# First unit's norm by sums that leave TensorE on all partitions, and its first loads on two queues

## The chip, the cores and the metric
One core of a Trainium2 chip runs the whole program. The metric is device time in microseconds of one execution; three runs of the kernel before gave 672.42, 673.34 and 673.81 us, median 673.34. Besides these there is one profiled execution, from which every duration below is read. Its engines are TensorE (PE, with weight loads as PEld), VectorE (DVE), ScalarE (ACT), GpSimd (POOL) and SyncE (SP), which issues loads.

## The reference
One layer of a diffusion backbone over 2048 latent positions and 256 context positions of width 1024, all in f32:

```python
mod = silu(c) @ w_ada + b_ada            # shift, scale, gate
h   = rmsnorm(x, gain) * (1 + scale) + shift      # the same for ctx with c_ctx
uf, gf, ul, gl = split(h @ w_in)         # 512 columns each
yf = real(fft2(uf)) @ w_four             # over positions and group channels
yl = bidirectional gated linear recurrence(conv4(ul)), started from the context's final state
x  = x + gate * (concat(yf * silu(gf), yl * silu(gl)) @ w_out)
out = rmsnorm(x, final_gain)
```

The change lies in the first `rmsnorm`: x times the reciprocal root of the mean square of its 1024 features plus 1e-6.

## The kernel before, in words
The latent positions are cut into four units of 512, the context is a fifth. In stage one a unit's x is held transposed: features on the 128 partitions, in four tiles (xt) of two feature blocks each, the 512 positions along the row. For each of the eight feature blocks k a unit goes through: x times the position's reciprocal root (`prep_x`), scale and shift by the modulation gn, sh (`prep_hi`, which gives h and its rounded part hl), the remainder of the split (`prep_lo`), a fold of h for the Fourier group (`fold_x`, eo), a store of h, the products pul with the weights wu (`mms_ul`) and ptt with the Fourier weights wf (`mms_tt`). Products in f32 are made from three rounded partial products (`mm3`).

During the first unit the weights are prepared too. For each k the adaLN block goes through part (`ada_part`), a copy psb, small sums o (`ada_sum`) and the additions that give sh and gn (`ada_fin`); the raw weight wr goes through wu and, by way of the matmuls pw (`four_mm`), through wf.

For units 1 to 3 and the context, the position sums of squares come from a second, untransposed load of x, whose squares ACT sums along the row. The first unit has no such load. Its squares are made from the xt tiles: ACT squares seven of the eight blocks, DVE the eighth; DVE adds blocks 0 to 3 into one tile, 4 and 5 into a second and 6 and 7 into a third (`square0`, `sum0`). TensorE then sums over partitions (`col0`): the tile of squares is the stationary operand, two columns of ones move, and the sums of 128 positions land on 128 partitions, four groups for 512 positions. Root and reciprocal (`stats`) are thus 4 columns wide. `spread` brings them back along the row: matmuls pr against the identity copy each value over all partitions. The first multiply reads pr in PSUM; `spread_copy` puts it into SBUF for the other seven.

The engines' order is written by hand: stage one is the list S1, whose words name operation, unit and block: X load of xt, a load of an adaLN block, w load of a weight, 1 square, + add, 3 column sum, ! warm-up matmul of TensorE with ones, 2 and 4 small ACT operations that also load its tables, A part, b psb, c o, d sh and gn, T root and reciprocal, P spread, x, h, l as above, i pw, m pul. Each engine takes its instructions in that order. SP issues nearly all loads, its queue in order; ACT issues only the load of the small vectors at the start. PSUM holds eight buffers in stage one, which these products take in turn.

Of the kernel before, what the change touches and what calls it, by code (L numbers as in the profile page):

```python
# [52 lines left out]
def tile_layer(ctx, tc, xp, xnat, xt_in, ctxn, ctxt, w_ada, vec, bgate, fgain, w_in, w_g, w_four, w_gate, w_out,  # L53
               dct, d512, rmat, csts, out):
    nc = tc.nc
# [11 lines left out]
    def r(ap):  # L67
        return ap.bitcast(F32)
# [23 lines left out]
    eps_r = const.tile([P, 1], F32, name="eps_r")  # L92
    b1 = const.tile([P, KD], F32, name="b1")
# [9 lines left out]
    p1 = p1stack.enter_context(tc.tile_pool(name="p1", bufs=1, reuse_waits="tile"))  # L103
# [3 lines left out]
    ident = p1.tile([P, P], F32, name="ident", tag="ident")  # L107
    ones_r = p1.tile([P, P], F32R, name="ones_r", tag="onesr")
# [85 lines left out]
    sts = {}  # L194
# [27 lines left out]
    def stats(u):  # L222
        n = 2 if u == "c" else 4
        st = p1.tile([P, 8], F32, name="st0", tag="st", bufs=3) if u == 0 else sts.pop((u, "st"))
        if u == 0:
            nc.scalar.activation(out=st[:, 4:4 + n], in_=sts["ss"][:, 0:2 * n:2], func=AF.Sqrt, scale=1.0 / D, bias=eps_t)
        else:
            nc.scalar.activation(out=st[:, 4:4 + n], in_=st[:, 0:n], func=AF.Sqrt, scale=1.0 / D, bias=eps_t)
        nc.vector.reciprocal(out=st[:, 0:n], in_=st[:, 4:4 + n])
        if u == 0:  # L230
            sts[u] = st
            return
        dgs = []
        if u:
            sr = p1.tile([P, 2, 4], F32R, name=f"sr{u}", tag="sr", bufs=2)
            nc.vector.tensor_copy(sr[:, 0, 0:n], st[:, 0:n])
            nc.vector.tensor_tensor(out=sr[:, 1, 0:n], in0=st[:, 0:n], in1=r(sr[:, 0, 0:n]), op=ALU.subtract)
            for s in range(2):
                dg = p1.tile([P, 4, P], F32R, name=f"dg{u}_{s}", tag="dg", bufs=2)
                nc.vector.tensor_tensor(out=dg[:, 0:n], in0=ident.unsqueeze(1).to_broadcast([P, n, P]),  # L240
                                        in1=r(sr[:, s, 0:n]).unsqueeze(2).to_broadcast([P, n, P]), op=ALU.mult)
                dgs.append(dg)
# [196 lines left out]
    nc.scalar.activation(out=eps_r, in_=eps_t, func=AF.Silu)  # L439
# [28 lines left out]
    def soft_abs():  # L468
# [6 lines left out]
        "!": warm_up, "0": const_loads, "9": small_loads, "1": square0, "+": sum0, "3": col0, "r": lambda: spread_copy(0),  # L475
# [17 lines left out]
    p2 = p2s.enter_context(tc.tile_pool(name="p2", bufs=1, side="right", reuse_waits="tile"))  # L493
# [4 lines left out]
    w4 = [fp.tile([P, 2, 512], F32R, name=f"w4_{j}", tag="w4", bufs=4) if j != 2 else  # L498
          fp.tile([P, 512], F32R, name="w4_2", tag="w42", bufs=1) for j in range(5)]
# [149 lines left out]
    X0 = CTX + GAP  # L649
# [371 lines left out]
    xs, pos, s3 = {}, {}, {}  # L1021
# [7 lines left out]
    p3 = tail.enter_context(tc.tile_pool(name="p3", bufs=1, reuse_waits="tile"))  # L1029
# [195 lines left out]
```

## Time and profile before

| | |
|---|---|
| median of three runs | 673.34 us |
| profiled execution | 675.62 us, span 673.5 us |
| TensorE busy | 659.3 us, 98% |
| VectorE busy | 477.2 us, 71% |
| ScalarE busy | 402.9 us, 60% |
| mean granted TensorE clock | 0.982 |
| HBM read, written | 91.24 MB, 38.27 MB |

Busy time of TensorE counts records whose ends are modelled, so 98% does not say that it runs at its peak; the granted clock beside it says whether it ran at 2.4 GHz (1.00) or 1.2 GHz (0.50). "Idle before" is the time for which an engine did nothing ahead of an instruction, with what released it. The chain follows the program back from its last instruction to what each step waited for.

### The profile page before, as it was taken

To read this page: it belongs to the slowest core of one execution; us is meant where nothing else is said; L and a number is where in the kernel's file an instruction comes from. 1 tells how busy PE (TensorE), PEld (TensorE's weight loads), DVE (VectorE), ACT (ScalarE), POOL (GpSimd) and SP (SyncE) were. 2 spreads that over 40 slices of the span, in tenths; PEclk is the share of its full clock that TensorE was granted. 3 is DMA by queue.
4 is the path that set the end of the run, shared out by engine and by line. 5 is a ranking of instruction groups with operands and counts; after the bars stand their busy time and mean duration, and the time that the engine had idled before them with its cause. 6 is when DMAs were issued, how large, how long until landed. Compare 5 with 4: busy or idle time off the path is not lost.

```text
span 673.5 us, 10726 instructions
## 1 busy us (share of the span) xinstructions
PE 659.3 (98%) x4124; PEld 578.8 (86%) x4124; DVE 477.2 (71%) x771; ACT 402.9 (60%) x578; POOL 105.4 (16%) x170
## 2 busy tenths in 40 slices
PE   8999999999989999999999999999999999999996
PEld 7888888888978889997998989989988888888885
DVE  3768999877646676487879899888989455544513
ACT  4475787556634455668587876887753455543502
POOL 0000201022130113333212222031210000000000
PEclk8899999999997999999999999999999999999998
DMA  9987785639695895344444353342479567774211
GB/s 339 396 315 260 222 293 170 238 94 283 133 328 174 246 315 149 127 126 115 151 116 145 106 184 110 111 141 73 139 254 338 199 219 234 239 255 177 93 63 62
DMA packets 69898, 130.21 MB, mean 193 GB/s; under 512 B 7090, under 2 KB 39986, under 8 KB 69848
## 3 DMA queue, kind: packets, MB, share of 16 engines
q1 hardware_dynamic: 51080, 82.36, 37.7%
q0 software_dynamic: 12384, 39.00, 17.7%
q10 hardware_dynamic: 6384, 8.18, 3.7%
q8 instruction: 32, 0.52, 0.3%
q14 instruction: 18, 0.15, 0.1%
HBM read 91.24 MB, written 38.27 MB: 192 GB/s over the span
## 4 chain that ended last, share of the span: by engine, by line
PE 92%; DMA 3%; ACT 2%; DVE 1%; issue 1%; SPq 0%; DVEq 0%; ACTq 0%
PE po L71 9%; PE pg L71 9%; PE po L72 9%; PE po L73 9%; PE pg L73 9%; PE pg L72 9%; PE pul L71 5%; PE pul L73 4%; PE pul L72 4%; PE ptt L71 2%; PE ptt L73 2%; PE ptt L72 2%; PE pl L72 2%; PE pl L73 2%; PE pl L71 2%; DMA w4a<-in_w_four_dram 1%
## 5 line engine op out<-in xcount | busy, mean ns | idle before, releaser
L71 PE MATMUL pg<-hg,wg 128*128 128x256 f32 x512 | 144.2, 282 | 0.7 <-ACT bs L636 0.7
L73 PE MATMUL pg<-hg,wg 128*128 128x256 f32 x512 | 143.8, 281 | 0.0
L72 PE MATMUL pg<-hg,wg 128*128 128x256 f32 x512 | 143.5, 280 | 0.0
L71 PE MATMUL po<-wo,y 128*128 128x512 f32 (+1 forms) x264 | 102.4, 388 | 0.0
L72 PE MATMUL po<-wo,y 128*128 128x512 f32 (+1 forms) x264 | 102.3, 387 | 0.0
L73 PE MATMUL po<-wo,y 128*128 128x512 f32 (+1 forms) x264 | 102.3, 387 | 0.0
L71 PEld LDWEIGHTS pg<-hg,wg 128*128 128x128 f32 x512 | 96.3, 188 | 4.0 <-ACT wg L544 1.1
L72 PEld LDWEIGHTS pg<-hg,wg 128*128 128x128 f32 x512 | 96.3, 188 | 0.7
L73 PEld LDWEIGHTS pg<-hg,wg 128*128 128x128 f32 x512 | 96.4, 188 | 0.0
L424 POOL DMA_DIRECT2D g_d<-gs x80 | 57.7, 723 | 138.4 <-ACT gs L744 63.3
L71 PEld LDWEIGHTS po<-wo,y 128*128 128x128 f32 x264 | 49.9, 189 | 11.0
L73 PEld LDWEIGHTS po<-wo,y 128*128 128x128 f32 x264 | 49.6, 188 | 11.2
L72 PEld LDWEIGHTS po<-wo,y 128*128 128x128 f32 x264 | 49.6, 188 | 10.7
L71 PE MATMUL pul<-hl,wu 128*128 128x512 f32 x124 | 49.9, 402 | 0.0
L1068 ACT ACTIVATE j<-xr 128x1024 bf16<-128x1024 f32 x15 | 15.9, 1057 | 55.6 <-DVE xr L1063 55.6
L73 PE MATMUL pul<-hl,wu 128*128 128x512 f32 x124 | 49.0, 395 | 0.0
L72 PE MATMUL pul<-hl,wu 128*128 128x512 f32 x124 | 48.8, 394 | 0.0
L838 ACT ACTIVATE g<-pl,vecs 128x1024 f32<-128x1024 f32 x32 | 35.5, 1116 | 14.3 <-PE pl L73 14.2
L287 ACT ACTIVATE h<-xt,sh,gn 128x512 f32<-128x512 f32 x31 | 25.2, 813 | 19.8 <-DVE gn L149 10.4
L71 PE MATMUL ptt<-wf,eo 128*128 128x260 f32 (+1 forms) x128 | 36.5, 286 | 0.0
L73 PE MATMUL ptt<-wf,eo 128*128 128x260 f32 (+1 forms) x128 | 36.3, 283 | 0.0
L72 PE MATMUL ptt<-wf,eo 128*128 128x260 f32 (+1 forms) x128 | 36.2, 283 | 0.0
(297 smaller groups left out, 1475.6 us busy)
## 6 DMA issues: line engine op xcount, KB each, us to landing
xt<-in_xt_dram SPq DMA_DIRECT2D x16, 512.0 KB, 5.4
blk<-in_w_ada_dram SPq DMA_DIRECT2D x16, 512.0 KB, 6.9
hr<-h_d SPq DMA_DIRECT2D x32, 256.0 KB, 4.2
xr<-in_xnat_dram SPq DMA_DIRECT2D x16, 512.0 KB, 3.8
g<-g_d SPq DMA_DIRECT2D x15, 512.0 KB, 5.4
out_dram<-xr POOLq DMA_DIRECT2D x15, 512.0 KB, 2.9
dm<-in_dct_dram POOLq DMA_DIRECT2D x12, 514.0 KB, 6.8
x<-in_xp_dram SPq DMA_DIRECT2D x12, 512.0 KB, 5.1
```

Of the source, the lines that this page charges most:

```text
L71: nc.tensor.matmul(out_, lh, rh, start=first, stop=False, skip_group_check=skip)
L72: nc.tensor.matmul(out_, lh, rl, start=False, stop=False, skip_group_check=skip)
L73: nc.tensor.matmul(out_, ll, rh, start=False, stop=last, skip_group_check=skip)
L287: nc.scalar.activation(out=h[:, 0:n], in_=x, func=AF.Identity, scale=g, bias=b)
L424: queue.dma_start(dst[:, :, row:row + s1 - s0], s[:, :, P * i - off + s0:P * i - off + s1])
L838: nc.scalar.activation(out=t[:, c0:c0 + cn], in_=pg[:, 0:cn], func=AF.Sigmoid, bias=vecs[:, q:q + 1])
L1068: nc.scalar.activation(out=junk, in_=xs[b][t], func=AF.Square, accum_out=s3[b, t][:, 0:1])
```

## The change
Four things are edited, all for the first unit. The column sums take the ones as the stationary operand and move the 512 columns of squares, so each of 128 partitions holds all 512 sums. Root and reciprocal are 512 wide, on that tile, and give rb itself. The spread's matmuls and rb's copy go. The second and fourth xt tile are loaded from ACT's queue; the small Silu that loads ACT's first table is put behind these issues (the word 8). In S1 the words P0 and r go and T0 comes behind b0.

```diff
-S1 = "X0.0 X0.1 X0.2 X0.3 9 a0.0 ... 32 A0 T0 P0 b0 x0.0 c0 d0 u0 h0.0 U0 a2.1 l0.0 f0.0 i0 e0.0 s0.0 r o0.0 ...
+S1 = "X0.0 X0.1 X0.2 X0.3 8 9 a0.0 ... 32 A0 b0 T0 c0 x0.0 d0 u0 h0.0 U0 a2.1 l0.0 f0.0 i0 e0.0 s0.0 o0.0 ...
...
     def load_xt(u, q):
-        nc.sync.dma_start(t[:, :, 0:n], ...)
+        queue = nc.scalar if u == 0 and q % 2 else nc.sync
+        queue.dma_start(t[:, :, 0:n], ...)
...
     def col0(j):
         if j == 0:
             sts["ss"] = ps1.tile([P, 512], F32, name="ss", tag="tr")
-        acc = sts["sq", (0, 4, 6)[j]]
-        for i in range(4):
-            nc.tensor.matmul(sts["ss"][:, 2 * i:2 * i + 2], acc[:, P * i:P * i + P], ones[:, 0:2],
-                             start=j + i == 0, stop=j == 2, skip_group_check=True)
+        nc.tensor.matmul(sts["ss"], ones, sts["sq", (0, 4, 6)[j]], start=j == 0, stop=j == 2)
...
     def stats(u):
         n = 2 if u == "c" else 4
-        st = p1.tile([P, 8], F32, name="st0", tag="st", bufs=3) if u == 0 else sts.pop((u, "st"))
         if u == 0:
-            nc.scalar.activation(out=st[:, 4:4 + n], in_=sts["ss"][:, 0:2 * n:2], func=AF.Sqrt, scale=1.0 / D, bias=eps_t)
...
+            t = rb[0] = p1.tile([P, 512], F32, name="rb0", tag="rb", bufs=2)
+            nc.scalar.activation(out=t, in_=sts["ss"], func=AF.Sqrt, scale=1.0 / D, bias=eps_t)
+            nc.vector.reciprocal(out=t, in_=t)
+            return
...
     def spread(u):
-        if u == 0:
-            for i in range(4):
-                nc.tensor.matmul(pr[:, P * i:P * i + P], sts[0][:, i:i + 1].to_broadcast([P, P]), ident, start=True, stop=True)
...
-        if u:
-            spread_copy(u)
+        spread_copy(u)
...
-    nc.scalar.activation(out=eps_r, in_=eps_t, func=AF.Silu)
...
+        "8": lambda: nc.scalar.activation(out=eps_r, in_=eps_t, func=AF.Silu),
```

The order of instructions shows it at three places. On ACT, at the program's start, before (vecs is the load of the small vectors, eps_r the table-loading operation, sq the squares):

```order
L76 DMA vecs<-in_vec_dram 128x92
L439 ACT_TABLE_LOAD
L439 ACTIVATE eps_r<-eps_t 128x1
L202 ACTIVATE sq_168<-xt_0_129 128x512
L202 ACTIVATE sq_170<-xt_0_129 128x512
```

and after:

```order
L76 DMA vecs<-in_vec_dram 128x92
L185 DMA xt_1_130<-in_xt_dram 128x1024
L185 DMA xt_3_134<-in_xt_dram 128x1024
L466 ACT_TABLE_LOAD
L466 ACTIVATE eps_r<-eps_t 128x1
L203 ACTIVATE sq_168<-xt_0_128 128x512
```

Two tile loads now stand between the vector load and the table load. On TensorE, from the last column sum (ss) to the first products of the unit (pul), before:

```order
L213 MATMUL ss<-ones,sq_185 128x2 x4
L131 MATMUL part_214<-blk_0_139,sc_pad 32x256 x4
L131 MATMUL part_214<-blk_1_141,sc_pad 32x256 x4
L250 MATMUL pr_226<-ident,st_223 128x128 x4
L143 MATMUL o_0_234<-cst,psb_231 128x2
L144 MATMUL o_0_234<-cst,psb_231 128x2
L169 MATMUL pw_251<-rmi,wr_143 128x128 x3
```

and after:

```order
L212 MATMUL ss<-sq_185,ones 128x512
L131 MATMUL part_205<-blk_0_139,sc_pad 32x256 x4
L131 MATMUL part_205<-blk_1_141,sc_pad 32x256 x4
L143 MATMUL o_0_219<-cst,psb_214 128x2
L144 MATMUL o_0_219<-cst,psb_214 128x2
L169 MATMUL pw_237<-rmi,wr_143 128x128 x3
```

The spread pr is gone, and one wide matmul stands for four narrow ones. On DVE, from the last add of squares to the operand of the first pul, before:

```order
L206 TENSOR_TENSOR sq_185<-sq_185,sq_187 128x512
L229 RECIPROCAL st_223<-st_223 128x4
L137 COPY psb_231<-part_214 128x256
L272 TENSOR_TENSOR xt_0_129<-xt_0_129,pr_226 128x512
L148 TENSOR_SCALAR sh<-o_0_234,vecs 128x2
L149 TENSOR_SCALAR gn<-o_0_234,b_82,vecs 128x2
```

and after:

```order
L207 TENSOR_TENSOR sq_185<-sq_185,sq_187 128x512
L137 COPY psb_214<-part_205 128x256
L225 RECIPROCAL rb_216<-rb_216 128x512
L263 TENSOR_TENSOR xt_0_128<-xt_0_128,rb_216 128x512
L148 TENSOR_SCALAR sh<-o_0_219,vecs 128x2
L149 TENSOR_SCALAR gn<-o_0_219,b_82,vecs 128x2
```

The reciprocal has moved behind psb, and 512 columns stand where 4 stood.

## Rows read from the trace of the kernel before
**Rows 1.** The page, chain that ended last: shares of the span by engine

```profile
PE 92%; DMA 3%; ACT 2%; DVE 1%; issue 1%; SPq 0%; DVEq 0%; ACTq 0%
```

**Rows 2.** Windows: stretch, its length, busy by engine, granted clock, DMA share, GB/s

```profile
1.00:4.00 3.00, 2.94 (x14) 2.95 (x15) 0.36 (x4) 1.49 (x2) 0.65 (x1) 1.00 0.65 144
5.00:7.50 2.50, 2.50 (x23) 2.34 (x21) 1.10 (x3) 2.07 (x4) 0.00 (x0) 1.00 1.04 413
...
11.00:12.00 1.00, 1.00 (x6) 0.92 (x6) 0.14 (x1) 0.36 (x2) 0.00 (x0) 0.55 1.01 414
12.00:21.00 9.00, 9.00 (x47) 7.42 (x48) 4.08 (x10) 2.08 (x4) 0.60 (x1) 0.50 1.03 418
21.00:22.00 1.00, 1.00 (x6) 0.85 (x5) 0.69 (x1) 1.00 (x3) 0.00 (x0) 0.83 1.01 414
...
199.00:209.00 10.00, 9.18 (x31) 7.34 (x31) 6.40 (x15) 4.04 (x11) 1.08 (x2) 0.50 0.78 257
```

**Rows 3.** Timeline, loads and squares: start, length, instruction, idle before and releaser

```profile
0.74 1.80 SPq L184 DMA_DIRECT2D xt<-in_xt_dram  x4
...
6.58 1.23 ACT L202 ACTIVATE sq<-xt 128x512 f32<-128x512 f32 x2 [0.16 <-DMA xt<-in_xt_dram]
...
7.86 1.15 ACT L202 ACTIVATE sq<-xt 128x512 f32<-128x512 f32 x2
...
8.80 1.05 PE L213 MATMUL ss<-ones,sq 128*128 128x2 f32 x8 [1.27 <-DVE sq L206]
9.04 0.69 DVE L206 TENSOR_TENSOR sq<-sq,sq 128x512 f32<-128x512 f32 x1 [0.30 <-ACT sq L202]
9.22 0.63 ACT L202 ACTIVATE sq<-xt 128x512 f32<-128x512 f32 x1 [0.21 <-DMA xt<-in_xt_dram]
...
10.44 0.69 DVE L206 TENSOR_TENSOR sq<-sq,sq 128x512 f32<-128x512 f32 x1
...
11.19 1.87 PE L213 MATMUL ss<-ones,sq 128*128 128x2 f32 x8
```

**Rows 4.** Timeline, from the root to the first pul, as rows 3

```profile
12.99 1.93 PE L131 MATMUL part<-blk,sc_pad 128*32 128x256 f32 x16
13.10 0.26 ACT L226 ACTIVATE st<-ss,eps_t 128x4 f32<-128x4 f32 x1 [1.73 <-PE ss L213]
...
14.85 2.08 PE L250 MATMUL pr<-ident,st 128*128 128x128 f32 x8
14.99 0.42 DVE L137 COPY psb<-part 128x256 f32<-128x256 f32 x1 [1.42 <-PE part L131]
...
16.96 0.69 DVE L272 TENSOR_TENSOR xt<-xt,pr 128x512 f32<-128x512 f32 x1 [1.55 <-PE pr L250]
...
17.43 2.38 PE L169 MATMUL pw<-rmi,wr 128*128 128x128 f32 x10
...
18.05 0.81 ACT L284 ACTIVATE hl<-xt,sh,gn 128x512 fp32r<-128x512 f32 x1 [4.18 <-DVE gn L149]
...
19.56 2.45 PE L334 MATMUL pul<-hl,wu 128*128 128x512 f32 x6
```

**Rows 5.** Groups of DVE by shape, reciprocals: count, busy us, mean ns, idle before

```profile
L1076 DVE RECIPROCAL s<-s 128x1 f32<-128x1 f32 x15 | 2.5, 165 | 32.1 <-ACT s L1072 32.1
L229 DVE RECIPROCAL st<-st 128x4 f32<-128x4 f32 x4 | 0.7, 177 | 2.3 <-ACT st L226 2.3
L443 DVE RECIPROCAL sp<-sp 128x8 f32<-128x8 f32 x1 | 0.2, 191 | 0.0
```

**Rows 6.** DMA queues in 2 to 5 us: packets, MB, share (q1 SP, q10 ACT)

```profile
q1 hardware_dynamic: 200, 0.75, 83.6%
q10 hardware_dynamic: 144, 0.05, 7.6%
```

**Rows 7.** Groups of ACT by shape, as rows 5: 512 columns with a scale operand

```profile
L535 ACT ACTIVATE w<-w4a,cst 128x512 fp32r<-128x512 f32 x2 | 1.4, 722 | 7.0 <-DVE w4a L532 7.0
```

**Rows 8.** Timeline of TensorE at the second low stretch, as rows 3

```profile
199.82 0.58 PE L71 MATMUL pz<-dm,S 128*126 128x256 f32 x1 [2.91 <-DVE z L617]
```

More of the change, by code (lines that the diff above doesn't have):

```diff
@@ new lines @@
+S1 = "X0.0 X0.1 X0.2 X0.3 8 9 a0.0 a0.1 w0 0 70 !21 10 11 +1 12 13 +2 +3 2 14 15 +5 16 17 4 +7 w1 30 a1.0 a1.1 a2.0 !1 31 !1 32 A0 b0 T0 c0 x0.0 d0 u0 h0.0 U0 a2.1 l0.0 f0.0 i0 e0.0 s0.0 o0.0 j0 w2 m0.0.0 i1 j1 J0 a3.0 J1 A1 u1 b1 4 w3 m0.0.2 U1 c1 d1 x0.1 h0.1 f0.1 e0.1 t0.0 a4.0 s0.1 l0.1 i2 x0.2 A2 b2 j2 u2 U2 o0.1 a3.1 m0.1.0 w4 c2 d2 J2 h0.2 m0.1.2 n1.0 f0.2 e0.2 a5.0 t0.1 w5 a4.1 o0.2 i3 l0.2 A3 b3 s0.2 n1.1 j3 J3 u3 q1.0 m0.2.0 x0.3 c3 d3 h0.3 a5.1 f0.3 e0.3 t0.2 s0.3 l0.3 U3 m0.2.2 i4 A4 b4 x0.4 6 j4 n1.2 J4 u4 o0.3 4 m0.3.2 q1.1 a6.0 m0.3.0 c4 t0.3 d4 a6.1 w6 h0.4 f0.4 U4 e0.4 l0.4 u5 i5 o0.4 j5 A5 b5 J5 a7.1 s0.4 U5 n1.3 q1.2 w7 a7.0 m0.4.0 x0.5 c5 d5 t0.4 h0.5 f0.5 e0.5 i6 x0.6 A6 l0.5 s0.5 b6 j6 u6 q1.3 U6 o0.5 T1 m0.4.2 u7 X1.0 J6 c6 d6 m0.5.2 h0.6 t0.5 f0.6 e0.6 m0.5.0 l0.6 i7 o0.6 s0.6 j7 A7 b7 J7 m0.6.0 c7 x0.7 m0.6.2 d7 U7 h0.7 f0.7 e0.7 l0.7 o0.7 P1 x1.0 x1.1 t0.6 h1.0 s1.0 f1.0 e1.0 s0.7 m0.7.0 l1.0 m0.7.2 F0.0 t0.7 X1.1 F0.1 o1.0 g0 F0.2 h1.1 F0.3 m1.0.0 f1.1 e1.1 s1.1 X1.2 G0 l1.1 n2.0 71 o1.1 p0.1 x1.2 p0.0 75 h1.2 72 f1.2 e1.2 m1.0.2 t1.0 x1.3 s1.2 l1.2 S1.1.0 n2.1 L1.1.0 m1.1.0 73 74 x1.4 t1.1 o1.2 m1.1.2 h1.3 f1.3 q2.0 e1.3 l1.3 o1.3 q2.1 h1.4 76 n2.2 x1.5 s1.3 f1.4 e1.4 s1.4 l1.4 h1.5 m1.2.0 o1.4 m1.2.2 77 q2.2 78 X1.3 x1.6 79 f1.5 t1.2 l1.5 e1.5 m1.3.2 o1.5 t1.3 s1.5 n2.3 m1.3.0 m1.4.2 x1.7 X2.0 710 q2.3 T2 m1.4.0 h1.6 f1.6 e1.6 s1.6 X2.1 l1.6 711 712 o1.6 t1.4 h1.7 f1.7 e1.7 l1.7 o1.7 t1.5 s1.7 m1.5.0 P2 x2.0 713 h2.0 714 x2.1 f2.0 s2.0 e2.0 m1.6.0 m1.5.2 715 l2.0 m1.7.0 x2.2 716 h2.1 m1.6.2 f2.1 o2.0 e2.1 m1.7.2 o2.1 n3.0 x2.3 t1.6 t1.7 F1.0 l2.1 F1.3 F1.2 717 F1.1 G1 g1 p1.0 718 h2.2 f2.2 e2.2 s2.1 p1.1 l2.2 s2.2 o2.2 m2.0.0 m2.0.2 S1.1.1 X2.2 719 n3.1 720 t2.0 x2.4 h2.3 q3.0 f2.3 e2.3 l2.3 o2.3 m2.1.0 t2.1 721 L1.1.1 n3.2 m2.1.2 t2.2 722 x2.5 723 s2.3 q3.1 X2.3 h2.4 f2.4 q3.2 m2.2.0 e2.4 l2.4 o2.4 x2.6 h2.5 m2.3.0 m2.2.2 f2.5 l2.5 e2.5 n3.3 724 s2.5 o2.5 m2.3.2 t2.3 q3.3 m2.4.2 725 x2.7 T3 t2.4 s2.4 h2.6 f2.6 X3.0 e2.6 l2.6 m2.4.0 h2.7 s2.7 726 m2.5.0 s2.6 f2.7 o2.6 e2.7 l2.7 P3 x3.0 o2.7 t2.5 x3.1 m2.5.2 t2.6 X3.1 m2.6.0 m2.6.2 h3.0 s3.0 f3.0 e3.0 l3.0 h3.1 x3.2 f3.1 s3.1 o3.0 e3.1 l3.1 o3.1 m2.7.0 F2.0 x3.3 m2.7.2 F2.2 t2.7 k F2.3 g2 F2.1 p2.1 X3.2 n4.0 h3.2 G2 f3.2 x3.4 p2.0 e3.2 l3.2 o3.2 s3.2 m3.0.0 m3.0.2 t3.0 h3.3 f3.3 e3.3 m3.1.0 q4.0 z2.0 n4.1 m3.1.2 m3.2.2 l3.3 s3.3 o3.3 S0.0.1 L0.0.1 x3.5 X3.3 m3.2.0 q4.1 h3.4 f3.4 e3.4 l3.4 t3.1 z2.1 s3.4 o3.4 h3.5 S0.1.1 x3.6 t3.2 f3.5 t3.3 e3.5 l3.5 S1.1.2 s3.5 m3.3.0 x3.7 m3.3.2 t3.4 m3.4.2 L0.1.1 X4.0 h3.6 T4 f3.6 h3.7 L1.1.2 s3.7 e3.6 l3.6 o3.5 o3.6 X4.1 s3.6 f3.7 e3.7 m3.4.0 o3.7 l3.7 m3.5.0 P4 m3.6.0 x4.2 x4.1 x4.0 m3.5.2 m3.6.2 h4.0 l4.0 x4.3 t3.5 h4.1 l4.1 h4.2 m3.7.0 m3.7.2 F3.0 X4.2 t3.6 F3.1 F3.2 l4.2 t3.7 F3.3 h4.3 g3 G3 X4.3 l4.3 p3.0 m4.0.0 m4.0.2 z3.0 p3.1 S0.0.0 x4.4 L0.0.0 x4.5 h4.4 m4.1.0 z3.1 S0.1.0 l4.4 L0.1.0 m4.1.2 x4.6 h4.5 l4.5 m4.2.0 S1.1.3 x4.7 m4.2.2 m4.3.2 L1.1.3 D0 h4.6 m4.3.0 l4.6 h4.7 m4.4.0 l4.7 D3 m4.4.2 m4.5.0 m4.5.2 m4.6.2 m4.6.0 m4.7.0 m4.7.2 F4.0 F4.1 F4.2 F4.3 G4".split()
@@ L183, in load_xt @@
         t = p1.tile([P, 2, 512], F32, name=f"xt{u}_{q}", tag="xt", bufs=XB)
-        nc.sync.dma_start(t[:, :, 0:n], ctxt[:, 2 * q:2 * q + 2, :] if u == "c" else xt_in[u, :, 2 * q:2 * q + 2, :])
+        queue = nc.scalar if u == 0 and q % 2 else nc.sync
+        queue.dma_start(t[:, :, 0:n], ctxt[:, 2 * q:2 * q + 2, :] if u == "c" else xt_in[u, :, 2 * q:2 * q + 2, :])
         xts[u, q] = t
@@ L223, in stats @@
         n = 2 if u == "c" else 4
-        st = p1.tile([P, 8], F32, name="st0", tag="st", bufs=3) if u == 0 else sts.pop((u, "st"))
         if u == 0:
-            nc.scalar.activation(out=st[:, 4:4 + n], in_=sts["ss"][:, 0:2 * n:2], func=AF.Sqrt, scale=1.0 / D, bias=eps_t)
-        else:
-            nc.scalar.activation(out=st[:, 4:4 + n], in_=st[:, 0:n], func=AF.Sqrt, scale=1.0 / D, bias=eps_t)
+            t = rb[0] = p1.tile([P, 512], F32, name="rb0", tag="rb", bufs=2)
+            nc.scalar.activation(out=t, in_=sts["ss"], func=AF.Sqrt, scale=1.0 / D, bias=eps_t)
+            nc.vector.reciprocal(out=t, in_=t)
+            return
+        st = sts.pop((u, "st"))
+        nc.scalar.activation(out=st[:, 4:4 + n], in_=st[:, 0:n], func=AF.Sqrt, scale=1.0 / D, bias=eps_t)
         nc.vector.reciprocal(out=st[:, 0:n], in_=st[:, 4:4 + n])
-        if u == 0:
-            sts[u] = st
-            return
         dgs = []
-        if u:
[L235 to L242, printed above, removed]
+        sr = p1.tile([P, 2, 4], F32R, name=f"sr{u}", tag="sr", bufs=2)
+        nc.vector.tensor_copy(sr[:, 0, 0:n], st[:, 0:n])
+        nc.vector.tensor_tensor(out=sr[:, 1, 0:n], in0=st[:, 0:n], in1=r(sr[:, 0, 0:n]), op=ALU.subtract)
+        for s in range(2):
+            dg = p1.tile([P, 4, P], F32R, name=f"dg{u}_{s}", tag="dg", bufs=2)
+            nc.vector.tensor_tensor(out=dg[:, 0:n], in0=ident.unsqueeze(1).to_broadcast([P, n, P]),
+                                    in1=r(sr[:, s, 0:n]).unsqueeze(2).to_broadcast([P, n, P]), op=ALU.mult)
+            dgs.append(dg)
         sts[u] = dgs
@@ L247, in spread @@
         pr = ps1.tile([P, 512], F32, name=f"pr{u}", tag="tr")
-        if u == 0:
-            for i in range(4):
-                nc.tensor.matmul(pr[:, P * i:P * i + P], sts[0][:, i:i + 1].to_broadcast([P, P]), ident, start=True, stop=True)
-        else:
-            for s, dg in enumerate(sts.pop(u)):
-                nc.tensor.matmul(pr[:, 0:P * n], ones_r, dg[:, 0:n].rearrange("p a b -> p (a b)"), start=s == 0, stop=s == 1)
+        for s, dg in enumerate(sts.pop(u)):
+            nc.tensor.matmul(pr[:, 0:P * n], ones_r, dg[:, 0:n].rearrange("p a b -> p (a b)"), start=s == 0, stop=s == 1)
         rb[u] = pr
-        if u:
-            spread_copy(u)
+        spread_copy(u)
     def spread_copy(u):
@@ L474, in tile_layer @@
     ops = {
-        "!": warm_up, "0": const_loads, "9": small_loads, "1": square0, "+": sum0, "3": col0, "r": lambda: spread_copy(0),
+        "!": warm_up, "0": const_loads, "9": small_loads, "1": square0, "+": sum0, "3": col0,
+        "8": lambda: nc.scalar.activation(out=eps_r, in_=eps_t, func=AF.Silu),
         "2": lambda: nc.scalar.activation(out=sc_pad[:, :, 0:2], in_=cc, func=AF.Silu),
```

1 line of the change is left out of this document (removed).

## The prediction
> **What bounds the kernel now.** I read the chain that ended last first: TensorE holds 92% of it [rows 1], so time leaves the program only where TensorE's stream is broken or slow. The change touches the first 20 us alone, so I then read the clock by stretches [rows 2]. The first two are the same warm-up matmuls: 14 passes in 3.0 us, then 23 in 2.5 us. The record prints 1.00 for both, but by this pace the full 2.4 GHz came between 4 and 5 us, 3 to 4 us after the work had begun at 1.06 (2.94 of the first 3.00 us are busy). At about 11.1 us the granted clock falls to half, 1.2 GHz (0.55 in the stretch 11:12), stays at 0.50 through 12:21 and is back at about 21.3 us (0.83 in 21:22). Before that fall TensorE had stood idle for 1.27 us, until 8.80, and then ran two-column matmuls [rows 3]. A second low stretch, 199:209, follows an idle of 2.91 us [rows 2, 8]. So the region of the change runs almost wholly at 1.2 GHz, and every 2 us of it gives back only 1 us of work.
>
> Third, the timeline of that region. The four x tiles arrive one by one; the second lets ACT go on at 6.58, the fourth at 9.22, both named as DMA waits, so the third is there at about 7.9 (midway). Each pair of squares follows its tile, DVE adds them up, and the sums pace the three column-sum steps on TensorE, the last at 11.19, ending at 13.06 [rows 3]. From there TensorE runs without a break: adaLN product (part) to 14.92, spread (pr) to 16.93, the small sums o, then pw from 17.43 to 19.81, then the first product of the unit, pul, at 19.8 [rows 4]. The operand hl was ready at 18.86, 0.95 us earlier: TensorE's own queue is what is late here, not the norm.
>
> **The change, part by part.** All terms are against the profiled execution (675.62 us with a span of 673.5; 2.3 us above the 673.34 median of the runs, so I add the sum to the median).
>
> *Column sums.* 12 matmuls with 2 moving columns become 3 with 512. The trace has no plain-f32 matmul with 512 columns; pw moves the same 512 columns in 5 pieces, 2.38 us at the low clock [rows 4], and the old step took 1.05 us at full and 1.87 at half clock [rows 3]. Two passes might as well cost half of that. I take no change, the old step's own 1.87 (bounds -0.9 to +0.5).
>
> *Spread.* The 8 pr passes leave TensorE: 2.08 us at the low clock [rows 4], all on the path. The PSUM copy of rb leaves ACT; it lies beside TensorE work and costs nothing.
>
> *Root and reciprocal, 512 wide.* The root reads PSUM on ACT; the nearest row with a scale operand is 722 ns [rows 7] against 0.26 us before [rows 4]: it lies beside part, so it is hidden (0). The reciprocal is the dear one. On DVE it takes 165, 177 and 191 ns for 1, 4 and 8 columns [rows 5], 3.5 to 4.0 ns for each further column. With 3.8 ns, 512 columns take 165 + 511 x 3.8 = 2.1 us, where an ordinary 512-wide DVE operation takes 0.69 [rows 3]. Bounds 0.69 and 165 + 511 x 4.0 = 2.2 us. It now stands behind psb on DVE (psb waits for part), so none of it lies beside part; x, gn and hl queue behind it.
>
> The Trainium skill speaks against the edit more strongly: "VectorE: DVE Perf Modes", section "First, the fixed hardware budget", says that reciprocal iterates its divide steps with a repeat count of 8. At one column per eight cycles of the 0.96 GHz that the page gives that would be an estimated 4.3 us, and the sum below would be 2.2 us worse. The rows of 1 to 8 columns grow at less than half that rate, so I do not take it as the forecast.
>
> *Loads on two queues.* SP's four issues take 1.80 us together [rows 3], 0.45 each; two of them move to ACT behind the vector load. That frees SP 0.9 us early, but TensorE waited for none of its later loads between 13.06 and 19.8 [rows 4]. What matters is how the tiles arrive. In 2:5 us both queues moved packets at once, 200 on SP's and 144 on ACT's, while the rate was shared [rows 6]. The ACT packets there are the vector load alone. After the change ACT's vector load still lies beside tile 0, so tile 0 comes as before; then tiles 1 and 2 share the engines, and both are there only at about 7.9, where before tile 1 came at 6.58. ACT's second pair of squares starts 1.3 us later, and ACT and DVE work back to back behind it (second pair 1.23 us, third 1.15, then the adds: the last add starts at 10.44, 1.40 after the one at 9.04 [rows 3]), so the last column sum moves by the same 1.3 us, to 12.5. Bounds: 0 if the tiles still arrive in order, and -0.45 if one issue slot is won; +1.3 at the top. I take 1.3, since the rows show sharing. ACT's table load also starts 0.9 us later, still over 2 us before the first square, and costs nothing.
>
> *Sum.* Last column sum 12.5, + 1.87 = 14.4; part + 1.86 = 16.2; psb + 0.07 + 0.42 = 16.7; reciprocal 18.8; x + 0.69 = 19.5; gn and the start of hl + 0.40 (as from 17.65 to 18.05 before); hl + 0.81 = 20.7 [rows 4]. TensorE has meanwhile done o and pw (16.7 to 19.8) and waits 1 us. pul starts at 20.75 instead of 19.8: +0.95 us. What is late next is the norm on DVE; it takes the place of TensorE's queue.
>
> *The clock behind it.* Before, pul ran 1.5 us at half clock until 21.3: 0.75 us of work lost. TensorE is now broken until 20.75. How soon the clock returns is bounded by rows: at the soonest at 21.3 as before; at the latest after as long an unbroken run as before (13.06 to 21.3 is 8.2 us, and 199.82 to about 209 is 9.2 us [rows 2, 8]), so at 29 to 30. The first rise came 3 to 4 us after dense matmuls began, and I take 3.4 of that: back at 24.15, 1.7 us of work lost, +0.95. Sum: 0.95 + 0.95 = +1.9 us, so 673.34 + 1.9 = **675.2 us**, with its own range of 673.8 (clock back at 21.3) to 678.1 (clock back at 30: 4.6 lost instead of 0.75, so +4.8).
>
> From 22 us on nothing is changed but PSUM buffers, and with TensorE 92% of the chain a shift of its start is carried to the end.
>
> **The rivals.**
> - *No change.* pul 0.95 late, but the clock returns at 21.3 as before: 0.95 + 0.28 - 0.75 = +0.5, 673.8. Or the tiles arrive in order: pul at 19.45, clock back 3.4 us later, -0.35 + 0.95 = +0.6, 673.9. For it: both low stretches were about 10 us long [rows 2]. Against it: both ended after an unbroken run.
> - *Faster: the 512-column sums keep the clock up.* The tiles come in order, the sums run at 2.4 GHz (11.19 + 1.05 = 12.2), part takes 0.93, psb ends at 13.7, the reciprocal at 15.8, hl at 17.7; pul starts at 17.75, 2.05 early, and the 0.75 lost before is saved too: -2.8, 670.5. If the clock falls in the 2.7 us wait for hl, it is -2.05 + 0.95 = -1.1, 672.2. For it: two-column matmuls are weak work, and they stood right before the fall. Against it: an idle of 1.27 us or more stays.
> - *Slower by the reciprocal.* If the wide instruction costs twice what its short rows show, 4.2 us, pul starts at 22.85: +3.05 + 0.95 = +4.0, 677.3. It decides from the point where reciprocal and multiply outlast o and pw, which is at about 1.1 us. The skill's repeat count, named above, is this case. Against it: the slope.
>
> That the second queue does not change how the tiles arrive is inside the first two.
>
> **How the numbers follow.** Forecast 0.40, no change 0.27, faster 0.23, dear reciprocal 0.10. About 0.2%, 1.35 us, can be told from no change. Slower by more: most of the forecast's range and the reciprocal, 0.48. Within: 0.30, with the forecast's lower end and the clock falling in the faster case. Faster by more: 0.22. The range that leaves out 2 in 10 runs from 671.2, inside the faster case, to 678.0, nearly at the forecast's upper end.
>
> **What would show it.** Right: the second pair of squares starts near 7.9 and the last column sum near 12.5; the 128x512 reciprocal takes 2.0 to 2.2 us; a TensorE idle of about 1 us stands before the first pul, released by hl; the clock is still at 0.50 after 21.3. Wrong: squares at 6.6, a granted clock of 1.00 through 12:18, a reciprocal of 0.7 us, or pul right behind pw.

## The result and the profile after

Fifteen executions of the changed kernel took 673.90 to 679.66 us, median 677.17; fifteen of the kernel before took 668.70 to 675.40, median 672.42. The ratio is 1.0065, 95% interval 1.0042 to 1.0087: slower by 4.4 us of 672.42. The profiled execution took 678.03 us with a span of 675.9, 2.4 us more than the one shown of before. That difference is the smaller one because the profiled execution of before was among its longest: it took 675.62 us, at a mean granted clock of 0.982.

The chain that ended last, after (shares of the span):

```profile
PE 92%; DMA 3%; ACT 2%; DVE 2%; issue 0%; SPq 0%; ACTq 0%; DVEq 0%
```

Against [rows 1] VectorE has one point more. The timeline of the loads, the squares and the column sums, after (start, length, instruction, idle before and its releaser):

```profile
0.74 0.86 SPq L185 DMA_DIRECT2D xt<-in_xt_dram  x2
...
1.19 0.93 ACTq L185 DMA_DIRECT2D xt<-in_xt_dram  x2
...
7.87 1.15 ACT L203 ACTIVATE sq<-xt 128x512 f32<-128x512 f32 x2 [1.88 <-DMA xt<-in_xt_dram]
...
9.03 1.65 ACT L203 ACTIVATE sq<-xt 128x512 f32<-128x512 f32 x3
...
10.08 1.13 PE L212 MATMUL ss<-sq,ones 128*128 128x512 f32 x2 [2.49 <-DVE sq L207]
...
11.28 1.92 PE L212 MATMUL ss<-sq,ones 128*128 128x512 f32 x2
...
13.42 1.64 PE L212 MATMUL ss<-sq,ones 128*128 128x512 f32 x2
```

Two of the four tile issues are now on ScalarE's queue. Against [rows 3] the second pair of squares starts at 7.87 instead of 6.58, after a DMA wait of 1.88 us, and the first column sum at 10.08 instead of 8.80, after an idle of TensorE of 2.49 instead of 1.27. The first sum takes 1.13 us; the second, begun as the clock fell, takes 1.92, and the third has to stand behind it. The same timeline from the root to the first pul:

```profile
15.09 0.69 ACT L224 ACTIVATE rb<-ss,eps_t 128x512 f32<-128x512 f32 x1 [2.89 <-PE ss L212]
...
16.12 0.42 DVE L137 COPY psb<-part 128x256 f32<-128x256 f32 x1 [3.83 <-PE part L131]
16.46 3.34 DVE L225 RECIPROCAL rb<-rb 128x512 f32<-128x512 f32 x1
...
17.07 1.31 PE L169 MATMUL pw<-rmi,wr 128*128 128x128 f32 x10
19.84 0.69 DVE L263 TENSOR_TENSOR xt<-xt,rb 128x512 f32<-128x512 f32 x1
...
20.89 0.81 ACT L275 ACTIVATE hl<-xt,sh,gn 128x512 fp32r<-128x512 f32 x1 [4.60 <-DVE gn L149]
...
21.75 2.93 PE L325 MATMUL pul<-hl,wu 128*128 128x512 f32 x6 [3.38 <-ACT hl L275]
```

Where [rows 4] had TensorE going from pw into pul without a break, pw now ends at 18.38 and pul starts at 21.75, behind 3.38 us of idle: hl waits for gn, which VectorE makes behind the multiply, and the multiply stands behind a reciprocal of 3.34 us. Windows of after (stretch, its length, busy by engine, granted clock, DMA share, GB/s):

```profile
1.00:26.00 25.00, 18.54 (x102) 14.16 (x106) 13.01 (x22) 10.11 (x18) 1.25 (x2) 0.86 0.98 382
11.00:12.00 1.00, 1.00 (x4) 0.58 (x3) 0.90 (x2) 0.99 (x2) 0.00 (x0) 0.61 1.04 426
12.00:14.00 2.00, 2.00 (x5) 1.10 (x4) 0.29 (x1) 0.20 (x1) 0.00 (x0) 0.50 1.04 410
15.00:18.00 3.00, 2.45 (x30) 1.80 (x29) 1.88 (x2) 1.19 (x2) 0.00 (x0) 1.00 1.04 425
18.00:21.00 3.00, 0.38 (x4) 0.24 (x3) 2.93 (x5) 0.12 (x1) 0.00 (x0) 1.00 1.02 419
21.00:25.00 4.00, 3.25 (x9) 2.67 (x10) 3.31 (x7) 1.80 (x3) 0.60 (x1) 0.57 1.02 419
```

and the first of these stretches in the kernel before:

```profile
1.00:26.00 25.00, 23.67 (x151) 20.76 (x152) 11.68 (x26) 11.57 (x21) 1.25 (x2) 0.80 0.99 381
```

One pair of rows holds the result: in the first 25 us TensorE is busy for 18.54 instead of 23.67 us, so it stands idle for 6.46 instead of 1.33, and this although its clock is higher (0.86 against 0.80). The low clock of [rows 2], 11 to 21 us in one piece, is now two shorter pieces: full clock is back before 15, and it is lost again soon after the stretch 18:21, in which TensorE is busy for 0.38 of 3 us.

The executions of one kernel differ by some 6 us, and most are listed with their span and mean granted clock. Two numbers separate the causes, roughly: span times clock, which is the span less what the low clock took from it, and the rest. For 35 executions of before (run beside the first four experiments) they average 662.3 and 7.4 us, for the 15 of after 667.2 and 7.4; for the 15 of before in the ratio no clocks are listed. By this the loss, here 4.9 us, is not a lower clock on average. It is time that the span gained at either clock, and the windows show TensorE idle in it.

The rest is only in part the clock of this stage. Each profile has a second low stretch near 200 us [rows 2], which no version touches. By the granted clock of windows of 1 us it takes 5.1 us from both profiled executions compared above, and from 1.7 to 6.8 in those of the experiments. Ahead of 32 us the low clock takes 5.1 us in before and 3.4 in after.

### The profile page after: what moved, and what is told of

It is laid out like the page before. It is cut to its first block, busy times and chain, and to the rows that moved or that the text cites. A ratio compares the mean times of both kernels' runs of the same rounds, so it can differ in the third digit from the quotient of the medians.

```text
span 675.9 us, 10667 instructions
## 1 busy us (share of the span) xinstructions
PE 657.0 (97%) x4098; PEld 574.3 (85%) x4098; DVE 480.2 (71%) x771; ACT 402.3 (60%) x577; POOL 105.4 (16%) x170
## 4 chain that ended last, share of the span: by engine, by line
PE 92%; DMA 3%; ACT 2%; DVE 2%; issue 0%; SPq 0%; ACTq 0%; DVEq 0%
PE po L71 9%; PE po L72 9%; PE pg L71 9%; PE po L73 9%; PE pg L73 9%; PE pg L72 9%; PE pul L71 4%; PE pul L72 4%; PE pul L73 4%; PE ptt L71 2%; PE ptt L73 2%; PE ptt L72 2%; PE pl L72 2%; PE pl L73 2%; PE pl L71 2%; DMA w4a<-in_w_four_dram 2%
```

## The experiments

For each the ratio to the kernel before, and the two averages just described (span times clock; rest).

| | ratio (95% interval) | span x clock | rest |
|---|---|---|---|
| the change | 1.0065 (1.0042 to 1.0087) | 667.2 | 7.4 |
| one queue | 1.0032 (1.0013 to 1.0051) | 665.1 | 6.4 |
| before with two queues | 1.0029 (1.0008 to 1.0050) | 663.8 | 8.2 |
| no reciprocal | 0.9985 (0.9965 to 1.0004) | 664.4 | 4.1 |
| the wait filled | 1.0023 (1.0006 to 1.0040) | 667.1 | 4.1 |
| one queue and the wait filled | 1.0005 (0.9987 to 1.0023) | 665.9 | 3.9 |
| reciprocal ahead of psb | 1.0127 (1.0097 to 1.0157) | 669.3 | 8.8 |
| before, 26 warm-ups | 1.0030 (1.0005 to 1.0055) | 663.6 | 7.8 |
| before, dense sums | 0.9989 (0.9967 to 1.0010) | 662.9 | 5.1 |
| before, dense sums, 26 warm-ups | 1.0008 (0.9989 to 1.0028) | 664.5 | 4.9 |

The 17 executions of before beside the 26 warm-ups gave 662.3 and 7.0, the 23 beside the dense sums 662.8 and 5.8, the 16 beside one queue and the wait filled 662.6 and 6.7: the rest varies by 1 to 2 us from one set to the next, so differences of it below 2 us say little.

### All tiles on one queue again

```diff
-        queue = nc.scalar if u == 0 and q % 2 else nc.sync
+        queue = nc.sync
```

> The changed kernel, but all four x tiles of the first unit go out on SyncE's queue again. Theory (the second queue lets tiles 1 and 2 share the engines and costs the squares 1.3 us): second pair of squares starts near 6.6 instead of 7.87 us, the first column sum near 8.8 instead of 10.08, the first pul near 20.4 instead of 21.75; time against before about 1.0045 or less instead of 1.0065. Rival (the tiles arrive late for another reason, or the queue is harmless because the wait is the reciprocal's): squares at 7.9 or pul still at 21.7, and 1.0065 unchanged.

Timeline of this kernel:

```profile
5.06 2.54 ACT L203 ACTIVATE sq<-xt 128x512 f32<-128x512 f32 x4 [2.38 <-DMA xt<-in_xt_dram]
...
8.58 1.13 PE L212 MATMUL ss<-sq,ones 128*128 128x512 f32 x2
...
18.80 2.93 PE L325 MATMUL pul<-hl,wu 128*128 128x512 f32 x6 [3.38 <-ACT hl L275]
```

Behind their first wait the first four squares run without another, the first sum starts 1.5 us earlier than in after, and the wait of 3.38 us before pul is there all the same. The ratio falls to 1.0032, about half of the loss. Its interval overlaps that of the change, but span times clock is lower by 2.1 us, more than twice the scatter of single executions (0.7 to 0.9). pul comes even 2.95 us earlier, more than expected, because in this execution the clock stayed up through the sums.

### The kernel before with two queues

```diff
-S1 = "X0.0 X0.1 X0.2 X0.3 9 a0.0 ...
+S1 = "X0.0 X0.1 X0.2 X0.3 8 9 a0.0 ...
...
-        nc.sync.dma_start(t[:, :, 0:n], ...)
+        queue = nc.scalar if u == 0 and q % 2 else nc.sync
+        queue.dma_start(t[:, :, 0:n], ...)
...
-    nc.scalar.activation(out=eps_r, in_=eps_t, func=AF.Silu)
...
+        "8": lambda: nc.scalar.activation(out=eps_r, in_=eps_t, func=AF.Silu),
```

> The kernel before, with only the loads changed: tiles 1 and 3 on ScalarE's queue, the small Silu behind them; narrow column sums, narrow reciprocal and spread as before. Theory (the queue costs 1.3 us by itself): second pair of squares near 7.9, last column sum near 12.5 instead of 11.19, first pul near 20.9 instead of 19.8, ratio to before 1.001 to 1.004. Rival (the queue is harmless alone, all the loss is the wide reciprocal): ratio 1.000, squares near 6.6.

```profile
7.86 1.15 ACT L203 ACTIVATE sq<-xt 128x512 f32<-128x512 f32 x2 [1.73 <-DMA xt<-in_xt_dram]
...
20.36 1.67 PE L335 MATMUL pul<-hl,wu 128*128 128x512 f32 x6 [0.22 <-ACT hl L285]
```

The second queue alone makes the old kernel slower, by 1.0029, and the squares are late by the same 1.3 us. The small Silu moved with the queue, but the squares waited for a DMA and not for it. So the queue costs time by itself, in either kernel.

### The reciprocal left out

```diff
-            nc.vector.reciprocal(out=t, in_=t)
+            nc.vector.tensor_scalar_mul(t, t, 1.0)
```

> The changed kernel with the 512-wide reciprocal left out (an ordinary 512-wide multiply by 1 stands in its place, so the norm is not computed). Theory (the reciprocal's 3.34 us makes the wait before the first pul): the multiply takes 0.4 to 0.7 us, pul starts near 19.0, the wait before it falls from 3.38 to under 1 us, the second fall of the clock at 21.5 us does not come, ratio to before 0.9995 to 1.002. Rival (what is lost is TensorE's low clock and not the wait for the norm): pul earlier, ratio still near 1.0065.

```profile
16.41 0.42 DVE L225 TENSOR_SCALAR rb<-rb 128x512 f32<-128x512 f32 x1
...
18.78 1.67 PE L325 MATMUL pul<-hl,wu 128*128 128x512 f32 x6 [0.45 <-ACT hl L275]
```

This version does not compute the norm; it only times the instruction. VectorE's instruction is 2.92 us shorter, and the wait of TensorE is shorter by 2.93. The ratio falls to 0.9985, with an interval wholly below that of the change: span times clock falls by 2.8 us, and the rest by 3.3. In this profile the clock does not fall again behind the wait (1.00 over 15:26), which in after took 1.7 us. So the reciprocal costs twice, once as a wait and once by the clock behind it; how much of the 3.3 us is the second, and how much the stretch near 200 us, these runs do not separate. With the cheap instruction the total is that of the kernel before within the interval, though span times clock is still 2.1 us higher: the lower rest makes up for it.

### The wait filled with warm-ups

```diff
-... o0.0 j0 w2 m0.0.0 i1 ...
+... o0.0 j0 w2 !14 m0.0.0 i1 ...
```

> The changed kernel with 14 more warm-up matmuls of TensorE between pw and the first pul, so that TensorE does not stand idle from 18.4 to 21.75 us; nothing else waits for them. Theory (the clock falls at 21.47 because of this wait): granted clock 1.00 from 14.6 us through 25, pul at 21.8 as before but running at full speed, 1.5 us less lost, ratio to before about 1.004 instead of 1.0065. Rival (the clock falls whatever stands in the wait, or its fall costs nothing that lasts): ratio 1.0065 unchanged.

```profile
12.19 1.12 PE L212 MATMUL ss<-sq,ones 128*128 128x512 f32 x2
...
16.48 3.34 PE L449 MATMUL warm<-ones 128*128 128x128 f32 x28
...
20.02 1.66 PE L325 MATMUL pul<-hl,wu 128*128 128x512 f32 x6 [0.20 <-ACT hl L275]
```

The 14 added warm-ups are 28 passes in the trace. pul takes 1.66 instead of 2.93 us. Span times clock is that of the change, to 0.1 us, and the rest falls from 7.4 to 4.1: useless matmuls in the wait give 2.8 us back (1.0023, an interval wholly below that of the change). In this execution the granted clock was 1.00 over 1:26, so here the third column sum stands at 12.19, near the 12.5 of the prediction.

### How long a reciprocal takes

```diff
+    junk = sc_pad.rearrange("p a b -> p (a b)")
+    for n in (16, 64, 128):
+        nc.vector.reciprocal(out=junk[:, 0:n], in_=ones[:, 0:n])
+    nc.vector.memset(sc_pad, 0.0)
```

> The changed kernel with three more reciprocals on VectorE at its start, of 16, 64 and 128 columns, on a tile of ones; nothing uses them. Theory (a constant cost for each column behind a start that short rows hide): 3.34 us for 512 columns is about 6.2 ns a column, so 128 columns take 0.85 to 0.95 us, 64 take 0.45 to 0.5, 16 about 0.2. Rival (3.8 ns a column as rows of 1 to 8 columns have it, and only long rows cost more): 128 columns 0.65 us, 64 columns 0.40, 16 columns 0.22.

This kernel ran once and serves for durations alone. Groups of VectorE by shape (count, busy us, mean ns, idle before):

```profile
L225 DVE RECIPROCAL rb<-rb 128x512 f32<-128x512 f32 x1 | 3.3, 3344 | 0.0
L1071 DVE RECIPROCAL s<-s 128x1 f32<-128x1 f32 x15 | 2.5, 164 | 32.1 <-ACT s L1067 32.1
L432 DVE RECIPROCAL sc_pad<-ones 128x128 f32<-128x128 f32 x1 | 1.0, 953 | 0.0
L432 DVE RECIPROCAL sc_pad<-ones 128x64 f32<-128x64 f32 x1 | 0.6, 553 | 0.0
L229 DVE RECIPROCAL st<-st 128x4 f32<-128x4 f32 x3 | 0.5, 177 | 0.1
L432 DVE RECIPROCAL sc_pad<-ones 128x16 f32<-128x16 f32 x1 | 0.3, 253 | 0.0
L437 DVE RECIPROCAL sp<-sp 128x8 f32<-128x8 f32 x1 | 0.2, 194 | 0.0
```

From 16 to 64 columns 300 ns are added, from 64 to 128 400, from 128 to 512 2391: 6.25, 6.25 and 6.23 ns for each column, and a line through them starts at 153 ns. From 1 to 8 columns only 30 ns are added, 4.3 a column: at 1 column the line would give 159 where 164 are measured, at 8 it would give 203 where 194 are. The short rows hold nearly nothing but the fixed part, and their slope is not that of the columns. The rows of 16 and 64 columns came 0.05 us above what was expected and that of 128 just above it; the rival's 0.65 us for 128 columns is far off.

### The reciprocal ahead of psb

```diff
-... A0 b0 T0 c0 x0.0 ... o0.0 j0 w2 m0.0.0 ...
+... A0 T0 b0 c0 x0.0 ... o0.0 j0 w2 !14 m0.0.0 ...
```

One queue and 26 warm-ups ahead of the sums went with it.

> The changed kernel with every cause found so far mended but the reciprocal's length: all x tiles on one queue, 26 warm-ups ahead of the sums, 14 between pw and the first pul, and the reciprocal ahead of psb on VectorE. Theory (the queue, the clock and the reciprocal's 3.34 us are all there is): last column sum near 11.0 us, reciprocal from 12.8 to 16.2, hl from 17.3 to 18.1, pul at 18.1 with the clock at 1.00 throughout, so 1.5 us before the 19.56 of the kernel before and about 0.8 us more from its pul at full clock: ratio 0.996 to 0.999. Rival (putting the reciprocal first delays psb, o and gn, which are then late instead): pul at 18.8 or later as with one queue, ratio 1.001 to 1.003.

```profile
11.59 1.02 PE L212 MATMUL ss<-sq,ones 128*128 128x512 f32 x2
...
13.38 3.35 DVE L225 RECIPROCAL rb<-rb 128x512 f32<-128x512 f32 x1 [2.61 <-ACT rb L224]
16.64 0.36 DVE L137 COPY psb<-part 128x256 f32<-128x256 f32 x1
...
17.06 0.59 PE L143 MATMUL o<-cst,psb 128*128 128x2 f32 x2 [3.44 <-DVE psb L137]
...
17.93 2.37 PE L169 MATMUL pw<-rmi,wr 128*128 128x128 f32 x10
...
20.11 4.88 PE L449 MATMUL warm<-ones 128*128 128x128 f32 x28
24.74 1.64 PE L325 MATMUL pul<-hl,wu 128*128 128x512 f32 x6
```

My expectation failed badly: 1.0127 over six executions where 0.996 to 0.999 was written. Behind the reciprocal psb is late, o waits 3.44 us for it, pw stands behind o, and the 28 warm-up passes, which were meant for a wait that had moved, now run for 4.88 us, at half clock at first (0.50 over 18:21), with pul behind them. The rival was right, and worse than it said. The place behind psb was the better one.

### One queue and the wait filled

```diff
-... o0.0 j0 w2 m0.0.0 i1 ...
+... o0.0 j0 w2 !14 m0.0.0 i1 ...
...
-        queue = nc.scalar if u == 0 and q % 2 else nc.sync
+        queue = nc.sync
```

> The changed kernel with two of its three losses mended and the reciprocal where the change put it, behind psb: all x tiles on one queue, and 14 warm-ups between pw and the first pul. Theory (the failure of the version with the reciprocal ahead of psb came from psb, o and pw being held up, with the warm-ups behind them): last column sum near 11, pw done near 15.5, warm-ups done before hl is, first pul near 18.5 with the clock at 1.00; the gains of the two single mendings add up (1.0065 less 0.0033 and 0.0042), so ratio 0.997 to 1.001. Rival (warm-ups and one queue get in each other's way whatever the order): first pul at 20 or later, ratio above 1.003.

```profile
10.80 1.13 PE L212 MATMUL ss<-sq,ones 128*128 128x512 f32 x2
...
13.33 3.34 DVE L225 RECIPROCAL rb<-rb 128x512 f32<-128x512 f32 x1
...
18.62 1.67 PE L325 MATMUL pul<-hl,wu 128*128 128x512 f32 x6 [0.19 <-ACT hl L275]
```

The two mendings give 1.0005 (pul at 18.62, expected near 18.5). Added up, the gains of the single ones would give 0.9990, which lies inside the interval. So the failure above did not lie in one queue with a filled wait. What it had besides is the order and five more warm-ups ahead of the sums; its last sum started at 11.59 instead of 10.80, and its pul 6.1 us later, so most of it is the order with what stood behind it.

### The clock of the kernel before

Three versions of before, to see whether its early low clock can be had away:

```diff
-... 70 !21 10 ...
+... 70 !26 10 ...
```

> The kernel before with 26 warm-up matmuls instead of 21 ahead of the column sums, so that TensorE does not stand idle for 1.27 us before the first of them; the two-column sums stay. Theory (the first fall of the clock follows the idle): granted clock 1.00 through 12:18 us, the last sums 1.05 instead of 1.87 us, first pul near 17 instead of 19.56, ratio to before 0.994 to 0.998. Rival (the two-column matmuls are too little work, whatever stands before them): clock falls near 11 us as before, ratio 1.000.

Timeline, and windows in the columns used above:

```profile
8.66 0.95 PE L213 MATMUL ss<-ones,sq 128*128 128x2 f32 x8
...
18.66 2.91 PE L334 MATMUL pul<-hl,wu 128*128 128x512 f32 x6
```

```profile
1.00:26.00 25.00, 24.95 (x164) 22.16 (x164) 11.96 (x28) 11.67 (x21) 1.25 (x2) 0.80 0.98 377
12.00:18.00 6.00, 6.00 (x36) 4.71 (x37) 2.51 (x7) 1.70 (x3) 0.00 (x0) 0.50 1.04 419
```

The second moves 128 columns of ones where two were moved (the root reads every 128th sum):

```diff
-            nc.tensor.matmul(sts["ss"][:, 2 * i:2 * i + 2], acc[:, P * i:P * i + P], ones[:, 0:2],
+            nc.tensor.matmul(sts["ss"][:, P * i:P * i + P], acc[:, P * i:P * i + P], ones,
...
```

> The kernel before with one number changed: the column sums move 128 columns of ones instead of 2, so the 12 matmuls move as many columns as the three wide ones of the changed kernel, but the sums still land on 128 partitions; narrow root, narrow reciprocal and spread stay, and the idle of 1.27 us ahead of the first sum too. Theory (two-column sums let the clock fall at 11 us, and dense ones keep it): granted clock 1.00 through 12:18 us in most executions, first pul near 17, mean clock 0.992 to 0.995, ratio to before 0.994 to 0.998. Rival (what falls is set by the idle and by chance, and dense sums only cost their columns): clock falls as before, ratio 1.000 to 1.002.

```profile
12.39 0.18 DVE L229 RECIPROCAL st<-st 128x4 f32<-128x4 f32 x1 [1.55 <-ACT st L226]
12.99 1.16 PE L250 MATMUL pr<-ident,st 128*128 128x128 f32 x8
...
13.99 0.28 PE L143 MATMUL o<-cst,psb 128*128 128x2 f32 x2
...
14.35 1.31 PE L169 MATMUL pw<-rmi,wr 128*128 128x128 f32 x10
16.10 1.67 PE L334 MATMUL pul<-hl,wu 128*128 128x512 f32 x6 [0.44 <-ACT hl L284]
```

```profile
1.00:26.00 25.00, 24.34 (x191) 21.23 (x192) 14.85 (x34) 14.55 (x26) 1.80 (x3) 1.00 0.98 379
```

The third has both edits:

> The same dense sums on the kernel before, and 26 warm-ups instead of 21 ahead of them, so that idle and narrow matmuls are both gone. Theory (either alone lets the clock fall, as the idle did in the changed kernel and the narrow sums did with 26 warm-ups): mean clock 0.993 to 0.996, first pul near 17, ratio 0.993 to 0.997 and below that of the dense sums alone. Rival (26 warm-ups hold up the sums where the clock rises late, which made the kernel before 1.003 with them): ratio 1.000 to 1.003.

With 26 warm-ups TensorE does not stand idle ahead of the sums, yet in the profiled execution the clock fell (0.50 over 12:18, pul 2.91 us long) and the ratio is 1.0030: an idle is not needed for the fall. With dense sums the profiled execution kept 1.00 through 26 us, and pul started at 16.10 instead of 19.56; but over twelve executions the ratio is 0.9989 with 1 inside the interval, and the rest is 5.1 against 5.8 us of the before runs beside it. Dense sums with 26 warm-ups (1.0008) are no better, and the expected 0.994 to 0.998 did not come. The average of the rest is a weak test of the early fall: in the profile with dense sums and 26 warm-ups the clock stayed at 1.00 through 26 us, and the stretch near 200 us alone took 6.8 us.

The profiles sort better, one execution each. With two-column sums the clock fell in all three, at 11 to 12 us, behind an idle ahead of the first sum of 1.27 us (before), of 2.15 (before with two queues) and of none (26 warm-ups). With sums of 128 or 512 columns it stayed up in the six with an idle of 1.21 us or less (the wait filled) and fell in the three with 2.49 to 2.55 (the change, no reciprocal, the reciprocals of other widths). Two pairs stand closest. With 26 warm-ups and no idle the clock fell with two-column sums and stayed up with 128 columns. The change and its version with the wait filled run the same instructions up to there, but the first 42 warm-up passes took 6.54 us in one and 7.67 in the other: behind an idle of 2.49 us the clock fell, behind 1.21 it stayed up. That suits the theory written down for the third version, that either lets the clock fall. But it is one execution each, and narrow sums did not always go with a fall: single executions of before had a rest of 1.3 us in all, too little for one. So what decides the early fall stays open. No version that computes the norm is shown to beat the kernel before; the dense sums come nearest to it.

## Why the prediction was right in its sign and too small in its size

The prediction said slower by 1.9 us, by the wait of TensorE for hl that takes the place of its own queue. The sign and the mechanism held; the measured loss is 4.4 us. The median of 677.17 lies inside the forecast's own range of 673.8 to 678.1, but partly by luck: its upper part was there for a clock that stays low until 30 us, and what filled it was a longer wait. By its steps:

*Two queues: right.* 7.9 was forecast for the second pair of squares and 7.87 came; 1.3 us was the price. The tiles did share: the trace of after has 4.1, 6.6 and 7.6 us (least, median, most) from issue to landing of the four, so by an estimate the second and third, issued near 1.2 us, both landed at 7.7 to 7.8. At full clock pul starts at 18.62 with one queue and at 20.02 with two, 1.40 us apart (the wait filled in both), and the queue alone put before at 1.0029.

*Column sums: a little short.* No change was taken. At full clock a sum takes 1.02 to 1.13 us as the narrow ones did (0.95 to 1.05). In the profile the sums at half clock stood behind each other, so the last came at 13.42 instead of 12.5; this went as soon as the clock was back, since part took 1.07 us instead of 1.93. part, psb and the start of the reciprocal then came at 14.98, 16.12 and 16.46, against a forecast of 16.7 for the last.

*Spread: right at half clock.* Its 8 passes took 2.08 us there, but take 1.16 at full clock, where the change saves that much less.

*Reciprocal: mis-sized.* 2.1 us was forecast, with 2.2 as the upper bound from rows; 3.34 was measured. The bound was no bound: it carried the slope of 1 to 8 columns, 3.5 to 4.0 ns, out to 512 [rows 5], where 6.25 is what a column costs. The Trainium skill, "VectorE: DVE Perf Modes", section "First, the fixed hardware budget", gives a repeat count of 8, from which 4.3 us was estimated. The traces do not agree with that reading of it, eight cycles a column: 6.25 ns are six cycles of the 0.96 GHz that the Trainium skill's page gives. The estimate was still nearer than the rows. The rival of a dear reciprocal, 677.3 us, came nearer to the median of 677.17 than the forecast of 675.2, but by luck in part: its price of 4.2 us was too high, and it missed the loss of the cover, which is next.

*What is late at the start: the failing step.* "TensorE's own queue is what is late here, not the norm" was read from one execution, in which TensorE ran at half clock. That execution lies at the end of its list: its rest is 12.1 us, where the 35 average 7.4 and go from 4.0 to 11.4, so most others cannot have lost as much. There o and pw took 3.1 us (16.72 to 19.81) and hid the norm. At full clock they take 1.7 (13.99 to 15.66 in the dense-sum version), and the old norm is itself late by 0.44. The cover in which the reciprocal was to hide was the low clock's. That and the reciprocal's length make up the wait: 3.38 us where 0.95 was forecast. Of the difference, 1.24 is the longer instruction and 1.31 the shorter cover (o and pw took 1.78 us, from 16.60 to 18.38, not 3.09), less 0.14 by which the reciprocal started ahead of o. At full clock throughout, the old norm (with dense sums) starts pul at 16.10, the wide norm at 18.62 and the wide norm with two queues at 20.02: 3.92 us in all, against 2.19 between the two profiled executions (19.56 and 21.75). In the runs span times clock grew by 4.9; where the remaining 1 us of that comes from is not shown.

*The clock behind it: wrong in its course, and nothing in the mean.* Half clock was forecast without a break until 24.15, 0.95 us more lost. What came were two pieces, the second after the wait of 3.38 us, and over the executions the rest is 7.4 us before and after. So the sign named in advance, a clock of 0.50 after 21.3, came (0.57 over 21:25), but by a new fall. The cost of the wait's clock is real: 1.7 us in the profile, and 3.3 us of the average rest go when the wait is filled. But in the two profiles the change also shortened the low clock ahead of it, from 5.1 us lost to 1.7.

*The rivals.* The clock kept up through wide sums came in the profiles of four versions (one queue, the wait filled, both, the reciprocal ahead of psb), and none of the four is faster than the kernel before, since the reciprocal was then the bound. "No change" is ruled out by the interval, whose lower end is 1.0042.

## What to carry to other kernels

Before an operation is called hidden, ask at which granted clock its cover was profiled: cover made of TensorE work halves when the clock is up, and other executions of the same kernel may run so. A cost for a wide instruction is not to be carried out from rows of a few columns, which hold the fixed part alone; one row of 64 or 128 columns would have given 3.3 us. And what a spread by matmuls saves is compared whole: a reciprocal of 4 columns and the spread took 0.18 and 1.16 us at full clock, the wide reciprocal without spread 3.34.

## What was not expected of the hardware

- A reciprocal on VectorE takes 153 ns and 6.25 ns for each column, eight times the 0.42 us of an ordinary multiply at 512 columns of the same tile.
- A second queue brought the second x tile later: its first user starts at 7.87 us in the changed kernel and at 7.86 in the one before, instead of 6.58 [rows 3], and the squares of the changed kernel end at 10.68 instead of 9.85.
- Up to the wait, the changed kernel and its version with the wait filled run the same instructions; the granted clock fell to half at about 11 us in the one profiled execution and stayed at 1.00 in the other. With 26 warm-ups and TensorE busy for 24.95 of 25.00 us from 1 to 26 it still fell, to a mean of 0.80 in that stretch.
- 28 warm-up passes in a wait of 3.4 us kept the clock at 1.00 in the profile, and the average rest fell by 3.3 us; 28 passes in the wrong place stood for 4.88 us ahead of pul.
- Every profile has a low stretch near 200 us, in a part that no version touches, and it took from 1.7 us (one queue and the wait filled) to 6.8 (dense sums, 26 warm-ups).
